# Scan of a hybrid SSD and attention layer: gated y kept in place, one norm per group, four transpositions moved into the next group

## The chip, the cores and the metric

The kernel runs on one core of one Trainium2 chip. Its time is the device time of one execution in microseconds (us); for each kernel the median of several executions is compared. The kernel before took 1962.46 us in the median of three runs (1960.18 to 1966.06).

## The reference

The layer takes a residual stream of 512 positions by 2048 channels. One input projection of the normalised stream feeds two branches, a bidirectional Mamba-2 scan (SSD) and a latent attention; both are projected, weighted, summed, projected again and added to the input. The change touches the end of the scan branch only, in float32:

```python
y_fwd = ssd_scan(xs, dtf, a_f, bm, cm)
y_bwd = flip(ssd_scan(flip(xs), flip(dtb), a_b, flip(bm), flip(cm)))
y = y_fwd + y_bwd + d_skip[:, None] * xs
y = y.reshape(b, s, D_SSM) * silu(z_ssm)
y = rmsnorm(y.reshape(b, s, SSM_GROUPS, D_SSM // SSM_GROUPS), ssm_norm_w)   # 4 groups of 512 channels
merged = sigmoid(g_ssm) * (y @ w_proj_ssm) + sigmoid(g_attn) * (o @ w_proj_attn)
```

`rmsnorm` divides each row of 512 channels by the root of its mean square plus 1e-6. The sequence is worked in four chunks of 128 positions.

## The kernel before

The program first normalises and transposes the input (`h_h`, `h_l`, a high and a low part, so that three products make one of float32), then makes the gates, then runs the scan as four groups of 512 channels (`ssd_group`, called for g = 0 to 3), then the attention and the output projections. The scan has little work for TensorE (PE); long products of the input projection are laid between its steps. They stand in a queue of generators (`Fill`), each a tile of 48 products (`xbc`, `qkv`, `za`; lines 169 to 171), and the program says after each step of the scan how many are run: `gap()` a planned share, `bit(n)` at least n. The order on PE is the order in which the program is written (PE is scheduled by hand); the other engines are ordered by the scheduler from the program order and from priorities (`tc.high_priority`), and every engine then works its list in order. An instruction that waits therefore holds all that stands behind it on its engine.

One group goes like this.

- First stretch. A `gap()`, then PE transposes the tile `BT` (`post_b`, line 1016) and, after six products each, four tiles `xs` (`post_x`). These go to PSUM tiles of the tag `pb`, of which there are two, used in turn. ScalarE (ACT) copies each out (`b_h`, line 1021; `xT`, line 1027), and VectorE (DVE) makes `b_l` from the first.
- State stretch. Three steps of the states (`loc`, `off`). ACT sets the accumulator `yo` to the skip term (line 1115, eight instructions), POOL adds to it (line 1094).
- Diagonal stretch. For each chunk c and half q a decay matrix `G` is made on DVE and ACT, and PE multiplies it with `xT` into `yb` (`diag`, line 1167). At q = 1 the chunk is whole: DVE adds `yo` and `yb` into a fresh tile `y` (line 1170, tag `yz`, two buffers), and `y_norm` follows at once: DVE multiplies by the gate `z` (line 965), ACT squares with a row sum (line 967), DVE scales the sum (line 968), `small_rsqrt` takes the root on ACT (line 186, which needs a table load of its own) and the reciprocal with one Newton step on DVE (lines 188 to 192), and ACT scales `y` (line 969).
- `y_turn` transposes a normalised chunk: four transpositions on PE into a `pb` tile (line 975), four scalings on ACT into `yt` (line 979) and one store from ACT's queue (line 289). A list `turns` holds chunks whose transposition is owed. Two are paid in the diagonal stretch, beside `diag`, one before the last `diag`, and the fourth in the next group's state stretch.

After groups 1 and 2 the program also takes the norm of the query or key/value latents (`r_sum`): PE sums the squares over partitions (line 353, tile `rp`), DVE adds the epsilon (line 355, tile `vv`, 128x512), and `small_rsqrt` works on all 512 columns (tiles `rt` and `rr`). After group 3 `fill.run(60)` and the last `y_turn` close the scan.

Of the kernel before, what the change touches and what calls it, by code (L numbers as in the profile page):

```python
# [12 lines left out]
F32 = mybir.dt.float32  # L13
F32R = mybir.dt.float32r
I32 = mybir.dt.int32
AF = mybir.ActivationFunctionType
ALU = mybir.AluOpType
AX = mybir.AxisListType

P = 128  # L20
D = 2048
SEQ = 512
KT = D // P
TT = SEQ // P
# [8 lines left out]
EPS = 1e-6  # L33
# [40 lines left out]
def build(tc, a):  # L74
    nc = tc.nc
    act, dve, pool, pe = nc.scalar, nc.vector, nc.gpsimd, nc.tensor
# [20 lines left out]
    hi = open_pool("hi", side="right")  # L97
# [4 lines left out]
    def few(n):  # L102

        n_small[0] += n
        assert n_small[0] <= 96
        return small[:, n_small[0] - n:n_small[0]]
# [76 lines left out]
    def small_rsqrt(v, n, new):  # L183

        t = new("rt")
        act.activation(t, v, AF.Sqrt)
        r = new("rr")
        dve.reciprocal(r, t)
        dve.tensor_mul(t, r, r)
        dve.tensor_mul(t, t, v)  # L190
        dve.tensor_scalar(t, t, -0.5, 1.5, ALU.mult, ALU.add)
        dve.tensor_mul(r, r, t)
        return r
# [10 lines left out]
    for t in range(TT):  # L204
# [3 lines left out]
        for i, cs in enumerate(slice(*e) for e in zip(edges, edges[1:])):  # L208
# [3 lines left out]
            if i == 0:  # L212
                most, v, root, r = (few(1) for _ in range(4))
# [189 lines left out]
    fill = Fill()  # L403
# [514 lines left out]
    sw = open_pool("sw", reuse_waits="tile")  # L918

    for tag, n, shape in (("r", 6, [P, SEQ]), ("da0", 2, [P, 4, P]), ("da1", 2, [P, 4, P]), ("E", 2, [P, 4, P]),  # L920
                          ("G", 2, [P, 4, P]), ("cbf", 2, [P, P]), ("cbb", 2, [P, P]),
                          ("yz", 2, [P, SEQ]), ("yo", 1, [P, TT, SEQ]), ("xT", 1, [P, TT, SEQ])):
        for _ in range(n):
            sw.tile(shape, F32R if tag == "r" else F32, tag=tag, bufs=n, name=f"{tag}_place")

# [16 lines left out]
    ssz = few(16)  # L942
# [8 lines left out]
                i = qkv_left.pop(0)  # L951
                fill.add("qkv", qkv_gen(i, sq_q if i < 6 else sq_kv, tmp2))

    def rsqrt1(v):

        return small_rsqrt(v, 1, lambda n: hi.tile([P, 1], F32, tag={"rt": "mx", "rr": "nm"}[n], bufs=4, name=n))

    def z_load(c, g):
        z = st("z")
        nc.sync.dma_start(z, zs_d[c][g])  # L960
        return z

    def y_norm(c, g, y, z):

        dve.tensor_mul(y, y, z)
        s_ = ssz[:, 4 * c + g:4 * c + g + 1]
        act.activation(z, y, AF.Square, accum_out=s_)
        dve.tensor_scalar(s_, s_, 1.0 / 512, EPS, ALU.mult, ALU.add)
        act.activation(y, y, AF.Copy, scale=rsqrt1(s_))

    def y_turn(c, g, y):

# [11 lines left out]
    turns = deque()  # L984
# [18 lines left out]
    def ssd_group(g):  # L1003
# [20 lines left out]
        def post_x(ct, xs):  # L1024
            def f():
                tp = transposed(xs)
                act.copy(xT[:, :, ct * P:(ct + 1) * P], tp.rearrange("p (c k) -> p c k", c=TT))
            return f
# [16 lines left out]
        def bit(n):  # L1045
            left[0] += n - fill.run(n)
# [6 lines left out]
            bit(9)  # L1053
        post_b()
        for ct in range(4):
            bit(6)
            post_x(ct, xss[ct])()

        yo = sw.tile([P, TT, SEQ], F32, tag="yo", name="yo")
        yoh = yo.rearrange("p c (h k) -> p c h k", h=HPG)  # L1060
# [49 lines left out]
        for i in range(3):  # L1110
            with tc.high_priority(offset=30):
                ss = [state(0, i, nxt[0]), state(1, 3 - i, nxt[1])]
            if i == 0:
                for j in range(HPG):
                    act.activation(yoh[:, :, j], xTh[:, :, j], AF.Copy, scale=dsk[:, g * HPG + j:g * HPG + j + 1])
            if i < 2:
                nxt = [state_in(0, i + 1), state_in(1, 2 - i)]
            gap()
            if turns:
                y_turn(*turns.popleft())  # L1120
            offdiag(0, i + 1, ss[0])
            offdiag(1, 2 - i, ss[1])
            if i == 2:
                cb_make(0)
            gap()
# [34 lines left out]
        def diag(c, q, G):  # L1160

            if q == 0:
                ybs[c] = pc("yb")
            yb = ybs[c]
            for j in range(4):
                cs = slice((q * 4 + j) * 64, (q * 4 + j + 1) * 64)
                pe.matmul(yb[:, cs], G[:, j, :], xT[:, c, cs], start=True, stop=True)
            if q == 1:
                y = sw.tile([P, SEQ], F32, tag="yz", bufs=2, name="y")
                dve.tensor_add(y, yo[:, c], yb)  # L1170
                with tc.high_priority(offset=30):
                    y_norm(c, g, y, zs.pop(c))
                turns.append((c, g, y))

        last = None
        da_load(0, 0)
        for c in range(TT):
            for q in range(2):
                G = seg_make(c, q)
                if q == 0 and c < TT - 1:  # L1180
                    cb_make(c + 1)
                if (c, q) != (TT - 1, 1):
                    da_load(c + q, 1 - q)
                if q == 1:
                    zs[c] = z_load(c, g)
                gap()
                if q == 1 and len(turns) > 1:
                    y_turn(*turns.popleft())
                if last:
                    diag(*last)  # L1190
                last = (c, q, G)
# [1 line left out]
            loaded[g + 1] = group_loads(g + 1)  # L1193
        gap()
        gap()
        y_turn(*turns.popleft())
        diag(*last)

        if g == 2:
            put(rkv_d, r_sum(sq_kv, KL, tmp2))  # L1200
# [5 lines left out]
        ssd_group(g)  # L1206
    add_fill("za", len(za_left))
    ahead[0] = 150
    fill.run(60)
    y_turn(*turns.popleft())  # L1210
    close_pool("sw")
    close_pool("sp")

# [653 lines left out]
```

## Time and profile before

| | |
|---|---|
| median of three runs | 1962.46 us (1960.18 to 1966.06) |
| the profiled execution | 1964.5 us |
| its span in the trace | 1962.7 us |
| granted TensorE clock, mean | 0.998 |
| the scan in the trace | about 560 to 1096 us |
| last `diag` of group 0, 1, 2, 3 starts at | 696.76, 827.56, 950.50, 1081.06 us |
| ACT table loads for the root (line 186) | 16, of 1.28 us each |

Times in rows of the trace are us from the span's start; a row of the timeline gives start, duration, engine, line, operation, tiles, shape and count, and in brackets how long the engine idled before it and what released it. Products on PE overlap: a product of 128x512 is recorded with 0.39 us, though the next starts 0.23 us later. So the cost of a product is the distance of starts, and a row of idle time on PE is a lower bound of a wait.

### The profile page before, as it was taken

What the parts mean: (1) busy time and instruction counts of PE and PEld (TensorE: products, weight loads), DVE (VectorE), ACT (ScalarE), POOL (GpSimd) and SP (SyncE); (2) the same over time, 40 slices, a digit from 0 to 9 for tenths busy, and PEclk for the clock granted to TensorE, in tenths of its full rate; (3) what the DMA queues carried; (4) which work ended last, traced back from release to release, by engine and by line L of the source; (5) the groups of instructions that cost most, each with busy time, mean ns of one, the idle gap of its engine ahead of it and who ended that gap; (6) DMA issues with size and microseconds to landing.
All of it is one profiled execution on the core that took longest, in us unless ns stands there. A gap on an engine that the chain in (4) does not pass through costs nothing.

```text
span 1962.7 us, 24515 instructions
## 1 busy us (share of the span) xinstructions
PE 1926.9 (98%) x8834; PEld 1592.1 (81%) x8834; DVE 1462.4 (75%) x2064; ACT 1038.3 (53%) x1536; POOL 248.3 (13%) x317
## 2 busy tenths in 40 slices
PE   7999999999999999999999999999999999999998
PEld 5888888888878888878888888888877788888886
DVE  7986676776759869799786557676776899879467
ACT  6444444444455866757757444444455455444344
POOL 0001001001112021030210211111021111100011
PEclk9999999999999999999999999999999999999999
DMA  5469669668654554665554867887389687846437
GB/s 211 164 206 261 161 166 249 153 183 240 145 178 145 174 165 153 216 186 178 178 158 150 235 186 204 211 217 203 103 220 317 222 286 284 285 159 241 160 90 169
DMA packets 145785, 383.27 MB, mean 195 GB/s; under 512 B 16704, under 2 KB 34304, under 8 KB 145472
## 3 DMA queue, kind: packets, MB, share of 16 engines
q1 hardware_dynamic: 79104, 234.02, 35.7%
q0 software_dynamic: 30912, 103.82, 23.4%
q10 hardware_dynamic: 35648, 43.87, 6.3%
q8 instruction: 69, 1.13, 0.2%
q14 instruction: 52, 0.43, 0.1%
HBM read 329.55 MB, written 98.17 MB: 218 GB/s over the span
## 4 chain that ended last, share of the span: by engine, by line
PE 80%; DVE 9%; DMA 5%; issue 3%; ACT 2%; POOL 0%; SPq 0%; DVEq 0%; POOLq 0%; ACTq 0%
PE P L605 11%; PE P L606 11%; PE P L604 11%; PE xbc L169 3%; PE xbc L170 3%; PE za L169 3%; PE xbc L171 3%; PE za L171 3%; PE za L170 3%; PE qkv L171 2%; DVE wl L459 2%; PE qkv L169 1%; PE f L1626 1%; PE f L1625 1%; PE f L1627 1%
## 5 line engine op out<-in xcount | busy, mean ns | idle before, releaser
L458 ACT CAST wh<-X 128x1024 fp32r<-128x1024 f32 x164 | 172.5, 1054 | 199.5 <-PE P L606 157.8
L459 DVE TENSOR_TENSOR wl<-X,wh 128x1024 fp32r<-128x1024 f32 x164 | 199.7, 1222 | 84.8 <-ACT wh L458 84.2
L165 DVE TENSOR_TENSOR wl<-wraw,wh 128x1024 fp32r<-128x1024 f32 (+2 forms) x150 | 174.1, 1163 | 83.6 <-ACT wh L164 78.2
L164 ACT CAST wh<-wraw 128x1024 fp32r<-128x1024 f32 (+2 forms) x150 | 144.5, 967 | 116.3 <-PE za L170 32.1
L459 DVE TENSOR_TENSOR wl<-Y,wh 128x1024 fp32r<-128x1024 f32 x88 | 107.5, 1223 | 66.4 <-ACT wh L458 66.3
L458 ACT CAST wh<-Y 128x1024 fp32r<-128x1024 f32 x88 | 92.6, 1054 | 115.6 <-PE P L606 101.3
L169 PE MATMUL xbc<-h_h,wh 128*128 128x512 f32 x384 | 153.6, 400 | 0.0
L171 PE MATMUL xbc<-h_h,wl 128*128 128x512 f32 x384 | 150.1, 391 | 0.0
L170 PE MATMUL xbc<-h_l,wh 128*128 128x512 f32 x384 | 150.0, 391 | 0.0
L604 PE MATMUL P<-wh,h_h 128*128 128x512 f32 x384 | 149.4, 389 | 0.0
L605 PE MATMUL P<-wl,h_h 128*128 128x512 f32 x384 | 149.4, 389 | 0.0
L606 PE MATMUL P<-wh,h_l 128*128 128x512 f32 x384 | 149.4, 389 | 0.0
L458 ACT CAST wh<-wraw 128x1024 fp32r<-128x1024 f32 x68 | 71.6, 1054 | 110.6 <-PE P L606 58.5
L459 DVE TENSOR_TENSOR wl<-wraw,wh 128x1024 fp32r<-128x1024 f32 x68 | 83.0, 1221 | 59.5 <-ACT wh L458 59.4
L605 PE MATMUL P<-wl,S 128*128 128x512 f32 x288 | 112.1, 389 | 0.8 <-DVE wl L459 0.8
L606 PE MATMUL P<-wh,S 128*128 128x512 f32 x288 | 112.0, 389 | 0.0
L604 PE MATMUL P<-wh,S 128*128 128x512 f32 x288 | 112.0, 389 | 0.0
L169 PE MATMUL za<-h_h,wh 128*128 128x512 f32 x256 | 101.7, 397 | 0.0
L171 PE MATMUL za<-h_h,wl 128*128 128x512 f32 x256 | 99.9, 390 | 0.0
L170 PE MATMUL za<-h_l,wh 128*128 128x512 f32 x256 | 99.7, 389 | 0.0
L1377 ACT ACTIVATE pr<-s,nm 128x512 f32<-128x512 f32 x64 | 44.0, 688 | 79.1 <-DVE nm L1375 79.1
L171 PEld LDWEIGHTS xbc<-h_h,wl 128*128 128x128 f32 x384 | 72.4, 188 | 15.7
(746 smaller groups left out, 5084.8 us busy)
## 6 DMA issues: line engine op xcount, KB each, us to landing
wraw<-wi SPq DMA_DIRECT2D x102, 512.0 KB, 3.6
T_wps<-wps POOLq DMA_DIRECT2D x32, 512.0 KB, 11.0
da<-da_d SPq DMA_DIRECT2D x64, 256.0 KB, 4.0
T_wpa<-wpa POOLq DMA_DIRECT2D x32, 512.0 KB, 9.1
wraw<-wps SPq DMA_DIRECT2D x24, 512.0 KB, 6.2
wraw<-wo SPq DMA_DIRECT2D x20, 512.0 KB, 3.6
xbc_d<-xbc ACTq DMA_DIRECT2D x24, 256.0 KB, 2.9
wraw<-wun SPq DMA_DIRECT2D x16, 384.0 KB, 5.4
```

The source lines that it names most:

```text
L164: act.copy(h, raw)
L165: dve.tensor_sub(l, raw, h.bitcast(F32))
L169: pe.matmul(out, wh, xh, start=start, stop=False)
L170: pe.matmul(out, wh, xl, start=False, stop=False)
L171: pe.matmul(out, wl, xh, start=False, stop=stop)
L458: i = act.copy(hi_, raw)
L459: dve.tensor_sub(lo_, raw, hi_.bitcast(F32))
L604: pe.matmul(bs[i], xh, wh, start=(j == 0), stop=False)
L605: pe.matmul(bs[i], xh, wl, start=False, stop=False)
L606: pe.matmul(bs[i], xl, wh, start=False, stop=(j == 7))
L1377: act.activation(pr, s, AF.Exp, bias=nm, scale=SCALE, accum_out=sm_)
L1625: pe.matmul(acc, mh, wh, start=(start and k == 0), stop=False)
```

## The change

`y` has no tile of its own any more. DVE adds `yb` into `yo[:, c]` in place and multiplies by `z` there; ACT squares it with a row sum, as before. Root, reciprocal and Newton step are left out per chunk. When the fourth chunk of a group is gated, `y_norms` takes them once for four columns (`ssz[:, 4g:4g+4]`, into `yr`), and ACT scales the four chunks one after another. All four chunks are then owed to `turns`. They are paid in the first stretch of the next group: after each of the four `post_x`, one `y_turn`; between two of them stand nine products in place of six (`bit(9 if g else 6)`). The places in the state stretch, in the diagonal stretch and before the last `diag` have none any more. After group 3, `fill.run(45)` comes before the first `y_turn` and `fill.run(6)` after each. Nothing is left out of the computation.

```diff
--- before.py
+++ after.py
@@ -919,7 +919,7 @@
 
     for tag, n, shape in (("r", 6, [P, SEQ]), ("da0", 2, [P, 4, P]), ("da1", 2, [P, 4, P]), ("E", 2, [P, 4, P]),
                           ("G", 2, [P, 4, P]), ("cbf", 2, [P, P]), ("cbb", 2, [P, P]),
-                          ("yz", 2, [P, SEQ]), ("yo", 1, [P, TT, SEQ]), ("xT", 1, [P, TT, SEQ])):
+                          ("yo", 1, [P, TT, SEQ]), ("xT", 1, [P, TT, SEQ])):
         for _ in range(n):
             sw.tile(shape, F32R if tag == "r" else F32, tag=tag, bufs=n, name=f"{tag}_place")
 
@@ -951,22 +951,25 @@
                 i = qkv_left.pop(0)
                 fill.add("qkv", qkv_gen(i, sq_q if i < 6 else sq_kv, tmp2))
 
-    def rsqrt1(v):
-
-        return small_rsqrt(v, 1, lambda n: hi.tile([P, 1], F32, tag={"rt": "mx", "rr": "nm"}[n], bufs=4, name=n))
-
     def z_load(c, g):
         z = st("z")
         nc.sync.dma_start(z, zs_d[c][g])
         return z
 
-    def y_norm(c, g, y, z):
+    def y_gated(c, g, y, z):
 
         dve.tensor_mul(y, y, z)
-        s_ = ssz[:, 4 * c + g:4 * c + g + 1]
-        act.activation(z, y, AF.Square, accum_out=s_)
-        dve.tensor_scalar(s_, s_, 1.0 / 512, EPS, ALU.mult, ALU.add)
-        act.activation(y, y, AF.Copy, scale=rsqrt1(s_))
+        act.activation(z, y, AF.Square, accum_out=ssz[:, 4 * g + c:4 * g + c + 1])
+
+    yr = [few(4), few(4)]
+
+    def y_norms(g, ys):
+        s4 = ssz[:, 4 * g:4 * g + 4]
+        dve.tensor_scalar(s4, s4, 1.0 / 512, EPS, ALU.mult, ALU.add)
+        r = small_rsqrt(s4, 4, lambda n: yr[n == "rr"])
+        for c, y in enumerate(ys):
+            act.activation(y, y, AF.Copy, scale=r[:, c:c + 1])
+            turns.append((c, g, y))
 
     def y_turn(c, g, y):
 
@@ -1053,8 +1056,10 @@
             bit(9)
         post_b()
         for ct in range(4):
-            bit(6)
+            bit(9 if g else 6)
             post_x(ct, xss[ct])()
+            if turns:
+                y_turn(*turns.popleft())
 
         yo = sw.tile([P, TT, SEQ], F32, tag="yo", name="yo")
         yoh = yo.rearrange("p c (h k) -> p c h k", h=HPG)
@@ -1116,8 +1121,6 @@
             if i < 2:
                 nxt = [state_in(0, i + 1), state_in(1, 2 - i)]
             gap()
-            if turns:
-                y_turn(*turns.popleft())
             offdiag(0, i + 1, ss[0])
             offdiag(1, 2 - i, ss[1])
             if i == 2:
@@ -1166,11 +1169,9 @@
                 cs = slice((q * 4 + j) * 64, (q * 4 + j + 1) * 64)
                 pe.matmul(yb[:, cs], G[:, j, :], xT[:, c, cs], start=True, stop=True)
             if q == 1:
-                y = sw.tile([P, SEQ], F32, tag="yz", bufs=2, name="y")
-                dve.tensor_add(y, yo[:, c], yb)
-                with tc.high_priority(offset=30):
-                    y_norm(c, g, y, zs.pop(c))
-                turns.append((c, g, y))
+                y = yo[:, c]
+                dve.tensor_add(y, y, yb)
+                y_gated(c, g, y, zs.pop(c))
 
         last = None
         da_load(0, 0)
@@ -1184,8 +1185,6 @@
                 if q == 1:
                     zs[c] = z_load(c, g)
                 gap()
-                if q == 1 and len(turns) > 1:
-                    y_turn(*turns.popleft())
                 if last:
                     diag(*last)
                 last = (c, q, G)
@@ -1193,8 +1192,9 @@
             loaded[g + 1] = group_loads(g + 1)
         gap()
         gap()
-        y_turn(*turns.popleft())
         diag(*last)
+        with tc.high_priority(offset=60):
+            y_norms(g, [yo[:, c] for c in range(TT)])
 
         if g == 2:
             put(rkv_d, r_sum(sq_kv, KL, tmp2))
@@ -1206,8 +1206,10 @@
         ssd_group(g)
     add_fill("za", len(za_left))
     ahead[0] = 150
-    fill.run(60)
-    y_turn(*turns.popleft())
+    fill.run(45)
+    while turns:
+        y_turn(*turns.popleft())
+        fill.run(6)
     close_pool("sw")
     close_pool("sp")
```

The scheduler's order shows the move. On PE, from the last `diag` of group 1 to the first stretch of group 2, before (`cst` is the identity in a transposition, the sum's matrix of ones in `rp`; `xbc` and `qkv` are products of the fill, of which only the first of a run is kept):

```order
L975 MATMUL turn<-cst,y 128x128 x4
L1167 MATMUL yb<-xT,G 128x64 x4
L353 MATMUL rp<-sq_q,cst 128x512
L169 MATMUL xbc<-h_h,wh 128x512
...
L1016 MATMUL pb<-cst,BT 128x128 x4
...
L1016 MATMUL pb<-cst,xs 128x128 x4
...
L1016 MATMUL pb<-cst,xs 128x128 x4
```

And the same place now:

```order
L1170 MATMUL yb<-xT,G 128x64 x4
L353 MATMUL rp<-sq_q,cst 128x512
L169 MATMUL xbc<-h_h,wh 128x512
...
L1019 MATMUL pb<-cst,BT 128x128 x4
...
L1019 MATMUL pb<-cst,xs 128x128 x4
L978 MATMUL turn<-cst,yo 128x128 x4
...
L1019 MATMUL pb<-cst,xs 128x128 x4
L978 MATMUL turn<-cst,yo 128x128 x4
```

The transposition of a gated chunk now stands right behind the first `xs`. Between the last `diag` and `BT` stand 12 products in both (15 after groups 0 and 2), between `BT` and the first `xs` six before and nine now.

On DVE, the same place before, from the addition of the last chunk on:

```order
L1170 TENSOR_TENSOR y<-yo,yb 128x512
L355 TENSOR_SCALAR vv<-rp 128x512
L965 TENSOR_TENSOR y<-y,z 128x512
L188 RECIPROCAL rr<-rt 128x512
L968 TENSOR_SCALAR small<-small 128x1
L1022 TENSOR_TENSOR b_l<-pb,b_h 128x512
L189 TENSOR_TENSOR rt<-rr 128x512
L188 RECIPROCAL rr<-rt 128x1
L165 TENSOR_TENSOR wl<-wraw,wh 128x1024
L189 TENSOR_TENSOR rt<-rr 128x1
```

And now, from the epsilon of `r_sum` to the last step of the four-column reciprocal (the rows on `small` are `y_norms`, those on `rr`, `rt` and `vv` are `r_sum`):

```order
L355 TENSOR_SCALAR vv<-rp 128x512
L968 TENSOR_SCALAR small<-small 128x4
L188 RECIPROCAL rr<-rt 128x512
L188 RECIPROCAL small<-small 128x4
L1025 TENSOR_TENSOR b_l<-pb,b_h 128x512
L189 TENSOR_TENSOR small<-small 128x4
L189 TENSOR_TENSOR rt<-rr 128x512
L190 TENSOR_TENSOR small<-small 128x4
L190 TENSOR_TENSOR rt<-rt,vv 128x512
L191 TENSOR_SCALAR small<-small 128x4
L191 TENSOR_SCALAR rt<-rt 128x512
L192 TENSOR_TENSOR small<-small 128x4
```

The two chains are interlaced in both, and the 512-column reciprocal stands ahead of the small one in both; after group 2 the order is the same, with one `wl` (line 165) inside.

On ACT, the same place now:

```order
L962 ACTIVATE z,small<-yo 128x512
L186 ACT_TABLE_LOAD
L186 ACTIVATE rt<-vv 128x512
L186 ACTIVATE small<-small 128x4
L1024 CAST b_h<-pb 128x512
L1030 COPY xT<-pb 128x4x128
L971 ACTIVATE yo<-yo,small 128x512 x4
L289 DMA rq_d<-rr 128x512
L982 ACTIVATE yt<-turn,vec 128x128 x4
```

The four scalings stand in a row, behind the first `xT` copy and ahead of the first four scalings into `yt`. After group 0 there is no `r_sum`; there the order is the square, `b_h`, the table load, the root, one `wh` cast (line 164), the four scalings, and then the first `xT` copy.

## The prediction

> **What bounds the kernel now.** I read the page first, then the waits of PE inside the scan, then the rows around the end of a group.
>
> ```profile
> PE 1926.9 (98%) x8834; PEld 1592.1 (81%) x8834; DVE 1462.4 (75%) x2064; ACT 1038.3 (53%) x1536; POOL 248.3 (13%) x317
> PE 80%; DVE 9%; DMA 5%; issue 3%; ACT 2%; POOL 0%; SPq 0%; DVEq 0%; POOLq 0%; ACTq 0%
> ```
>
> PE is busy for 98% of the span and carries 80% of the chain that ended last. Work taken from ACT or DVE is worth nothing by itself here; what counts is whether PE waits more or less. In the window of the scan (560 to 1140 us) its waits are these:
>
> ```profile
> PE pb L1016 <- ACT dec L346: 2.6, 1, 2.6
> PE qkv L171 <- DVE wl L165: 2.1, 2, 1.3
> PE off L170 <- DVE s_l L1085: 0.7, 1, 0.7
> ```
>
> The first stands at the very start of the scan, which the change leaves as it is. So all that a lighter ACT and DVE could give back is 2.1 + 0.7 = 2.8 us. Of what the change can take there is no such limit: every wait that it puts into PE's list counts in full, since the products behind it are only shifted.
>
> **PE's side of the new place.** The change removes no product and no transposition from PE. It moves four transpositions per group to the next group's first stretch. The first is the one to look at: it needs the first scaled chunk, and that needs the square of the last chunk. When would PE get there? The rows of PE after groups 0, 1 and 2:
>
> ```profile
> 696.76 1.00 PE L1167 MATMUL yb<-xT,G 128*128 128x64 f32 x8
> ...
> 701.11 0.60 PE L1016 MATMUL pb<-cst,BT 128*128 128x128 f32 x4
> 702.94 0.60 PE L1016 MATMUL pb<-cst,xs 128*128 128x128 f32 x4
> ...
> 827.12 0.60 PE L975 MATMUL turn<-cst,y 128*128 128x128 f32 x4
> 827.56 1.00 PE L1167 MATMUL yb<-xT,G 128*128 128x64 f32 x8
> ...
> 832.06 0.60 PE L1016 MATMUL pb<-cst,BT 128*128 128x128 f32 x4
> 833.89 0.60 PE L1016 MATMUL pb<-cst,xs 128*128 128x128 f32 x4
> ...
> 955.69 0.60 PE L1016 MATMUL pb<-cst,BT 128*128 128x128 f32 x4
> 957.52 0.60 PE L1016 MATMUL pb<-cst,xs 128*128 128x128 f32 x4
> ```
>
> ```profile
> 641.30 0.39 PE L169 MATMUL xbc<-h_h,wh 128*128 128x512 f32 x1
> 641.53 0.39 PE L170 MATMUL xbc<-h_l,wh 128*128 128x512 f32 x1
> ```
>
> A product takes 0.23 us from start to start. From `BT` to the first `xs`, with six products, it is 1.83 us in all three places; with nine it becomes 1.83 + 3 x 0.23 = 2.5. Four transpositions take 827.56 - 827.12 = 0.44 us. On the clock of these rows PE reaches the first moved transposition at 701.11 + 2.5 + 0.44 = 704.1 after group 0, at 835.0 after group 1, at 958.6 after group 2. (The transposition that stood ahead of the last `diag` is gone, but that shifts both sides.)
>
> **The norm's side, after group 0.**
>
> ```profile
> 702.35 1.28 ACT L186 ACT_TABLE_LOAD   x1
> 703.65 0.20 ACT L186 ACTIVATE rt<-small 128x1 f32<-128x1 f32 x1
> 704.22 1.05 ACT L164 CAST wh<-wraw 128x1024 fp32r<-128x1024 f32 x1
> 705.17 0.73 ACT L969 ACTIVATE y<-y,rr 128x512 f32<-128x512 f32 x1
> 704.66 0.16 DVE L192 TENSOR_TENSOR rr<-rr,rt 128x1 f32<-128x1 f32 x1
> ```
>
> The order on both engines is the same up to the root, so the small reciprocal is ready at 704.66 + 0.16 = 704.8. On ACT the `wh` cast now follows the root directly and ends about 703.85 + 1.05 = 704.9. The first scaling takes 0.73: chunk 0 is ready at 705.6. PE waits 1.5 us. Behind this stand three more scalings, one `xT` copy and four scalings into `yt`, and only then is the `pb` tile free that the second `y_turn` needs: 704.9 + 4 x 0.62 + 0.5 + 1.14 (the four `yt`, row below) = 709.0. PE wants it at 705.6 + 0.44 + 2.5 = 708.6, and waits 0.4. I take 2.0 us, bounds 1.2 and 2.6.
>
> ```profile
> 698.23 1.14 ACT L979 ACTIVATE yt<-turn,vec 128x128 f32<-128x128 f32 x4
> ```
>
> **After group 1** the latents' norm shares the engines.
>
> ```profile
> 830.51 0.68 DVE L355 TENSOR_SCALAR vv<-rp 128x512 f32<-128x512 f32 x1
> 831.11 0.68 DVE L965 TENSOR_TENSOR y<-y,z 128x512 f32<-128x512 f32 x1
> ...
> 834.33 3.35 DVE L188 RECIPROCAL rr<-rt 128x512 f32<-128x512 f32 x1 [2.54 <-ACT rt L186]
> ```
>
> ```profile
> 832.37 1.28 ACT L186 ACT_TABLE_LOAD   x1 [2.20 <-issue]
> 833.66 0.63 ACT L186 ACTIVATE rt<-vv 128x512 f32<-128x512 f32 x1
> ```
>
> The gate's product now stands ahead of `vv` and ends about 831.6; the square ends at 832.4, the table load at 833.7, and the wide root starts where it does now. So does the reciprocal of 512 columns, 3.35 us long, and the small one stands behind it in DVE's list. How long the rest takes is read after group 2, where the same chain ran without a disturbance:
>
> ```profile
> 957.12 3.38 DVE L188 RECIPROCAL rr<-rt 128x512 f32<-128x512 f32 x2 [2.04 <-ACT rt L186]
> ...
> 961.74 1.22 DVE L165 TENSOR_TENSOR wl<-wraw,wh 128x1024 fp32r<-128x1024 f32 x1
> 962.87 0.14 DVE L191 TENSOR_SCALAR rt<-rt 128x1 f32<-128x1 f32 x1
> ...
> 963.53 0.15 DVE L192 TENSOR_TENSOR rr<-rr,rt 128x1 f32<-128x1 f32 x1
> 963.65 0.43 DVE L191 TENSOR_SCALAR rt<-rt 128x512 f32<-128x512 f32 x1
> 964.11 0.69 DVE L192 TENSOR_TENSOR rr<-rr,rt 128x512 f32<-128x512 f32 x1
> ```
>
> From the start of the wide reciprocal to the end of the small chain: 963.68 - 957.12 = 6.56. After group 1 there is no `wl` in between (962.87 - 961.74 = 1.13 less), but one wide step more stands ahead (964.11 - 963.65 = 0.46): 5.9 us. So the four factors are ready at 834.35 + 5.9 = 840.3, the first scaling at 841.0, and PE, which stood ready at 835.0, waits 6.0 us. Bounds 5.0 and 8.5: in the present run the same steps ended only at 843.6, beside a slow one:
>
> ```profile
> 841.25 2.37 DVE L192 TENSOR_TENSOR rr<-rr,rt 128x512 f32<-128x512 f32 x2
> ```
>
> With 0.2 for the second `pb` tile: 6.2.
>
> **After group 2** the `wl` stays inside. On ACT the `yt` scalings of an older chunk no longer stand ahead of the root, so I let its table load start 0.4 us before the present 955.16, and the wide reciprocal with it:
>
> ```profile
> 955.16 1.28 ACT L186 ACT_TABLE_LOAD   x1
> ```
>
> The wide reciprocal starts at 956.7, the factors are ready at 956.7 + 6.56 + 0.46 = 963.7, chunk 0 at 964.4. PE stood ready at 958.6: 5.8 us, with the second tile 5.9. Bounds 5.0 and 6.5.
>
> **After group 3** 45 products (10 us) stand ahead of the first `y_turn`, and the chain, which took 705.9 - 696.8 = 9.1 us without `r_sum`, is hidden. But on ACT a `wh` cast (1.05), a table load (1.28) and a Silu (0.6) stand inside the first chunk's `yt` scalings. The third `y_turn` needs that `pb` tile 2 x 1.83 = 3.7 us after the first; ACT is done 0.5 + 0.55 + 1.05 + 1.28 + 0.6 + 0.55 = 4.5 us after it. 0.8 us, bounds 0 and 1.5.
>
> **The clock.** One wait of this size is in the trace already, the one of 2.6 us at the start:
>
> ```profile
> 574.00:576.00 2.00, 0.00 (x0) 0.00 (x0) 0.00 (x0) 1.97 (x4) 1.26 (x1) 0.99 1.02 406
> 576.00:578.00 2.00, 1.65 (x6) 1.55 (x7) 1.19 (x3) 1.27 (x4) 0.00 (x0) 0.50 0.06 23
> 578.00:580.00 2.00, 2.00 (x10) 1.53 (x9) 0.00 (x0) 1.00 (x3) 0.00 (x0) 0.65 0.00 0
> 924.00:926.00 2.00, 0.98 (x5) 0.48 (x3) 2.00 (x5) 1.96 (x4) 0.00 (x0) 1.00 0.89 275
> ```
>
> Behind PE's busy time and the others stands the granted clock: it fell to 0.50 and came back within 4 us. What PE did in that time cost 1.65 x 0.50 + 2.00 x 0.35 = 1.5 us more. The wait of 1.3 us at 924 us left it at 1.00. So I add 1.5 us to each of the two long waits (bounds 0 and 3), and nothing to the 1.5 us after group 0, which is nearer to the second (bounds 0 and 1.5). The Trainium skill, "TensorE: Matmul & The Clock Gate", section "What's actually happening", has the clock fall after one idle window of about 3.4 us, the windows running free; here it fell after 2.6 us, so the trace disagrees, and by the page a wait of 6 us would hold a whole window only about three times in four (an estimate from that page), 2.3 us in place of 3.0.
>
> **What is given back.**
>
> ```profile
> L186 ACT ACT_TABLE_LOAD x16 | 20.5, 1283 | 2.5 <-issue 2.2
> ```
>
> ACT is rid of 12 of the 16 table loads for the root, and DVE of 12 small chains; the waits of 2.8 us above stand where both were full. I take half of it, 1.4, bounds 0 and 2.8. The Trainium skill, "ScalarE: Activation LUTs", section "What ACT_TABLE_LOAD costs", adds a drain of about 1.38 us to each load of 1.28; the root at 703.65 starts right behind the load at 702.35, so the trace shows none, and by the page each of three waits would be 1.4 longer.
>
> **The sum.** 2.0 + 6.2 + 5.9 + 0.8 + 3.0 - 1.4 = 16.5 us. Against the profiled execution's 1964.5 that is 1981.0; the median of the runs is 2.0 below it, so 1979.0.
>
> **The rivals.**
>
> *The clock stays up.* The waits come, but the fill's products resume without a fall. For it: at 924 us it held. Against it: 2.6 us were enough at 574. 16.5 - 3.0 = 13.5: 1976.0.
>
> *A second wait in the state stretch.* The accumulator can be set anew only when the old one is transposed, so its eight instructions on ACT move behind the last `y_turn`, and the casts of the state queue up among them. For it: the second state's cast stands behind five of them in ACT's list, about 2 us. Against it: there are some 6 us of products between `loc` and the second `off`. If it comes in each of three groups at 2.5 us, 24: 1986.5.
>
> *No wait.* The norm is ready in time, or the products ahead cover it. For it: nothing in the rows after groups 1 and 2, where the present chain of one column ended at 963.68, 5 us after PE would stand ready. 1962.5.
>
> *Faster.* The norm is in time and the relief of ACT and DVE removes the 2.8 us and some lags too small for the list of waits; it decides from the point where the chain from the last `diag` to chunk 0 takes less than the 7.3 us (704.1 - 696.8) that PE needs to the first moved transposition. It took 9.1 without `r_sum`. Minus 5: 1957.5.
>
> **How the numbers follow.** Forecast 0.63, clock stays up 0.15, second wait 0.10, no wait 0.07, faster 0.05. The low end of the sum's bounds is 1.2 + 5.2 + 5.1 + 0 + 0 - 2.8 = 8.7, which gives 1971.2; the high end, with 2.6 + 8.7 + 6.6 + 1.5 + 4.5 (a fall after each of three waits) - 0 = 23.9, gives 1986.4 and takes in the second wait. The range is 1971 to 1987. About 0.3% (6 us) is what a measurement of this kernel can tell from no change: slower 0.88, within 0.07, faster 0.05.
>
> **What would show it.** In the profile after, PE's waits in the scan should have a group of the transposition waiting for ACT's scaling of `yo`, three times, some 14 us in all and 6 us the longest, with the granted clock at half behind the long ones. Table loads for the root should be 4. If that group is missing or below 3 us, the step that fails is the time at which PE reaches the transposition or the order on DVE; if it is there and the time is not 10 us longer, the waits were paid elsewhere before.

## The result, and the profile after

The changed kernel takes 1990.66 us in the median of five runs (1985.34 to 1996.98); the kernel before took 1963.39 us in five runs on the same chip. The ratio is 1.0131, 95% interval 1.0116 to 1.0146: slower by 27.3 us, where 16.5 had been forecast. The direction was right, the size was not: the range ended at 1987. One later execution of the changed kernel, at a mean granted clock of 0.753, took 2431 us; no figure below takes it in.

The page of the changed kernel (the profiled execution took 1997.0 us): its first line and the lines on the engines and on the chain that ended last:

```profile
span 1995.2 us, 24402 instructions
PE 1940.3 (97%) x8834; PEld 1600.7 (80%) x8834; DVE 1457.3 (73%) x1992; ACT 1012.7 (51%) x1505; POOL 251.4 (13%) x317
PE 80%; DVE 8%; DMA 7%; issue 3%; ACT 2%; POOL 0%; SPq 0%; ACTq 0%; DVEq 0%; POOLq 0%
```

ACT is busy for 26 us less and DVE for 5 us less, and the span is 32 us longer. DMA's share of the chain rose from 5% to 7%: a first sign that not only the norm is late. PE's waits in the scan and just behind it (560 to 1200 us; us in total, times, longest), the first seven rows:

```profile
PE turn L978 <- ACT yo L971: 12.6, 3, 5.9
PE pb L1019 <- ACT dec L346: 2.6, 1, 2.6
PE za L171 <- DVE wl L165: 1.8, 1, 1.8
PE loc L170 <- DVE xw_l L1074: 1.6, 1, 1.6
PE loc L169 <- ACT xw_h L1073: 1.3, 1, 1.3
PE turn L978 <- ACT yt L982: 1.0, 2, 0.9
PE loc L169 <- DVE tmp L1098: 0.8, 1, 0.8
```

The first row is the forecast: the first moved transposition waits for ACT's scaling of `yo`, three times. The second stood there before. The rows of `loc` (the state stretch, whose inputs are the tiles `xw`) and `za` (the fill behind the scan) were not forecast.

A list of waits misses what PE loses at a low clock. The next table therefore counts all of it: for each matmul of PE, the time to the start of the next one less the usual spacing of its kind (the median, 0.23 us for a product of 512 columns), summed over stretches. "Again" is a second profile of the same kernel, from the first experiment.

| stretch of the span, us | what lies there | before | after | again |
|---|---|---|---|---|
| 700 to 750 | first stretch of group 1 | 0.4 | 2.7 | 2.6 |
| 800 to 850 | first stretch of group 2 | 1.0 | 9.2 | 8.9 |
| 950 to 1000 | first stretch of group 3 | 0.6 | 8.8 | 8.6 |
| 850 to 900 | state stretch of group 2 | 1.7 | 8.3 | 4.8 |
| 1100 to 1200 | end of the scan, first loads of the attention | 0.0 | 5.2 | 8.3 |
| 750 to 800 and 900 to 950 | diagonal stretches of groups 1 and 2 | 3.6 | 1.1 | 0.9 |

The first three rows lose 18.7 us against before, the next two 11.8 (11.4 in the second profile), and the last gives 2.5 back. Of what is left of the 32 us between these two profiles, 2.9 lie in one low clock near 120 us, before the scan, which the second profile does not have in that size.

The granted clock in four windows of the changed kernel (us, then busy time and instructions of PE, PEld, DVE, ACT and POOL, the granted clock, DMA share, GB/s):

```profile
838.20:844.40 6.20, 0.35 (x4) 0.11 (x2) 6.00 (x11) 1.41 (x3) 0.00 (x0) 0.88 0.00 0
844.40:851.20 6.80, 6.80 (x25) 5.69 (x26) 1.23 (x1) 4.82 (x12) 0.00 (x0) 0.61 0.33 107
975.20:980.70 5.50, 0.23 (x4) 0.02 (x1) 5.47 (x12) 1.91 (x4) 0.00 (x0) 0.89 0.10 20
980.70:987.50 6.80, 6.80 (x25) 5.69 (x26) 0.29 (x1) 3.79 (x11) 0.00 (x0) 0.59 0.39 140
```

In the first and third, PE stands idle while DVE works through the norms. In the two behind them PE is busy throughout and gets 25 instructions done at a mean clock of 0.6. Where no long wait stands ahead, a stretch of the same length holds 39, as in the run with the reciprocal behind the norm, after group 0.

### The profile page after: what moved, and what is told of

Its sections match the earlier page's. It is cut to its first block, busy times and chain, and to the rows that moved or that the text cites. A ratio compares the mean times of both kernels' runs of the same rounds, so it can differ in the third digit from the quotient of the medians.

```text
span 1995.2 us, 24402 instructions
## 1 busy us (share of the span) xinstructions
PE 1940.3 (97%) x8834; PEld 1600.7 (80%) x8834; DVE 1457.3 (73%) x1992; ACT 1012.7 (51%) x1505; POOL 251.4 (13%) x317
## 4 chain that ended last, share of the span: by engine, by line
PE 80%; DVE 8%; DMA 7%; issue 3%; ACT 2%; POOL 0%; SPq 0%; ACTq 0%; DVEq 0%; POOLq 0%
PE P L605 11%; PE P L606 11%; PE P L604 11%; PE xbc L169 3%; PE xbc L170 3%; PE xbc L171 3%; PE za L169 2%; PE za L171 2%; PE za L170 2%; PE qkv L169 2%; PE qkv L171 2%; PE qkv L170 2%; PE f L1627 1%; PE f L1629 1%; PE f L1628 1%
## 5 line engine op out<-in xcount | busy, mean ns | idle before, releaser
L170 PEld LDWEIGHTS xbc<-h_l,wh 128*128 128x128 f32 x384 | 73.4, 191 | 14.8 <-issue 0.2
```

Source lines behind the costliest of these rows:

```text
L170: pe.matmul(out, wh, xl, start=False, stop=False)
```

## The experiments

Ratios are to runs of the kernel before on the same chip in the same batch.

| kernel | median us | ratio, 95% interval |
|---|---|---|
| the changed kernel again | 1991.2 | 1.0132 (1.0115 to 1.0149) |
| reciprocals into the diagonal stretch | 1992.9 | 1.0145 (1.0129 to 1.0160) |
| four sums of y held | 1985.6 | 1.0104 (1.0087 to 1.0121) |
| both | 1985.4 | 1.0108 (1.0093 to 1.0124) |
| all sums behind the first head | 1984.4 | 1.0087 (1.0071 to 1.0104) |
| the same, norm per chunk | 1972.5 | 1.0033 (1.0022 to 1.0043) |
| all sums behind the first head, reciprocal behind the norm | 1974.3 | 1.0038 (1.0025 to 1.0051) |
| kernel before, all sums behind the first head | 1964.3 | 0.9996 (0.9984 to 1.0008) |
| all sums behind the first head, transpositions later | 1971.3 | 1.0032 (1.0019 to 1.0044) |
| the same, reciprocal behind the norm | 1968.3 | 1.0017 (1.0006 to 1.0028) |
| the last one with six products | 1969.6 | 1.0030 (1.0018 to 1.0041) |
| six products, norm per chunk, reciprocal where the change has it | 1970.0 | 1.0022 (1.0013 to 1.0030) |

Three causes were to be told apart. Theory 1: the group's norm is late, with the latents' reciprocal ahead of it. Theory 2: POOL's list holds the state inputs (`xw`) up. Theory 3: the attention's first loads (tile `raw`) land late.

### Which waits come back

No edit.

> The changed kernel unaltered, profiled a second time, to see which of its waits come back. Theory 1 (norm of four chunks late, reciprocal of the compressed norm ahead of it) and theory 2 (a copy on POOL's list waits ahead of the state inputs of the third group) both expect about 1990.7 us, PE waits of about 1.6, 6.0 and 5.4 us at the first transposition of groups 1, 2 and 3, a low clock behind the two long ones, and some 5 us of PE waits near 883 to 893 us. Rival (noise of one execution): the waits near 883 us, the one of 1.9 us at 1153 us and the low clock near 130 us are gone.

The waits of PE in the second profile, same window:

```profile
PE turn L978 <- ACT yo L971: 12.6, 3, 5.9
PE za L171 <- DVE wl L165: 4.4, 1, 4.4
...
PE loc L169 <- DVE tmp L1098: 1.9, 1, 1.9
```

The first row is the same to 0.1 us. The two unforeseen places are there again, with other sizes (4.4 for 1.8 us at the weight, 1.9 for 3.7 at the state inputs). All three belong to the kernel.

### The reciprocals into the diagonal stretch

```diff
-        if g == 2:
-            put(rkv_d, r_sum(sq_kv, KL, tmp2))
-        if g == 1:
-            put(rq_d, r_sum(sq_q, QL, tmp2))
...
                 last = (c, q, G)
+                if (c, q) == (1, 0) and g > 1:
+                    put(*((rq_d, r_sum(sq_q, QL, tmp2)) if g == 2 else (rkv_d, r_sum(sq_kv, KL, tmp2))))
```

> The changed kernel with the compressed norms' wide reciprocals taken out of the group ends and put into the middle of the next group's diagonal stretch; nothing else moved by hand. Theory 1: the waits at the first transposition fall from 6.0 and 5.4 us to the 1.6 us of group 1, where no reciprocal stands ahead, and no low clock follows: 4.4 + 3.8 + 2 x 2.9 = 14 us less, about 1977 us. Rival (the scaling of four chunks is late by itself, whatever stands ahead): the waits stay above 4 us and the time above 1986 us. Theory 2 alone would leave the time at 1990 us, and its waits near 883 us stay here.

The waits of PE, 560 to 1250 us:

```profile
PE turn L978 <- ACT yo L971: 4.7, 3, 1.8
PE loc L169 <- ACT xw_h L1073: 4.3, 1, 4.3
PE za L171 <- DVE wl L165: 3.6, 1, 3.6
PE yb L1170 <- DVE G L1160: 3.0, 2, 2.6
PE loc L170 <- DVE xw_l L1074: 2.6, 3, 1.3
...
PE qkv L171 <- DVE wl L165: 1.9, 1, 1.9
```

The forecast of theory 1 for the place came true: 12.6 us of waits became 4.7, the longest 1.8. The forecast for the time did not: 1992.9 us. The wide reciprocal now stands in a stretch where DVE has no slack (`yb` waits 2.6 us for `G`, `qkv` 1.9 us for a weight), and the state inputs, reached earlier, wait longer: 4.3 and 1.3 us where it was 1.3 and 1.6. The gain was paid elsewhere.

### The sums of y held

```diff
-            pool.tensor_add(yo[:, c], yo[:, c], tmp)
+            last_off[:] = [pool.tensor_add(yo[:, c], yo[:, c], tmp)]
...
+    with tc.issue_after(last_off[0].ins):
         for step in sums(yn_d, slice(0, 2048)):
             for f in step:
                 f()
```

> The changed kernel with the four transfers that sum the stored y (the POOL copies and the accumulating one) held behind the scan's last instruction of POOL; nothing else moved by hand. Theory 2: the cluster of PE waits near 883 to 893 us goes, about 7 us less, 1983.5 us; the waits of 6.0 and 5.4 us stay. Rival (that cluster comes from ACT and DVE, late after the wait of 5.4 or 6.0 us and the low clock): the cluster stays and the time is about 1990 us. If the held transfers are missed later, up to 17 us come back behind the scan.

POOL's instructions in the state stretch of group 2, first of the changed kernel, then of the kernel before (start, length, instruction, and in brackets the idle time ahead of it and what ended it):

```profile
864.44 1.11 POOL L1420 DMA_DIRECT2D yn_S<-yn_x  x1
...
881.46 0.54 POOL L1417 DMA_DIRECT2D yn_S<-yn_S  x1 [10.47 <-DMA yn_S<-yn_x]
...
883.25 2.05 POOL L1070 TENSOR_TENSOR xw<-xT,wst 128x512 f32<-128x512 f32 x2
```

```profile
855.44 3.03 POOL L1065 TENSOR_TENSOR xw<-xT,wst 128x512 f32<-128x512 f32 x2
...
860.21 1.11 POOL L1418 DMA_DIRECT2D yn_S<-yn_x  x1
872.32 0.51 POOL L1415 DMA_DIRECT2D yn_S<-yn_S  x1 [11.00 <-DMA yn_S<-yn_x]
```

The stored chunks of `y` are summed in DRAM by transfers on POOL's queue. A copy of such a sum cannot be issued until the accumulating transfer has landed, 17.0 us after its issue (881.46 - 864.44), and POOL stands still for the last 10.47 us of it. In the kernel before POOL stands still about as long (11.00 us), but behind the last two `xw`. In the changed kernel the chunks of group 1 are stored together in the first stretch of group 2, so the sums become due while state inputs are still to come, and the copy stands ahead of the last two `xw`. PE needs them, through the casts, from 883.6 on.

With the sums held, that wait is gone from PE's list, which has 12.6 us at the transpositions, 2.9 at a weight behind the scan, and nothing of `loc`. The stretch from 850 to 900 us falls from 8.3 (4.8 in the second profile) to 1.1. The ratio falls from 1.0132 to 1.0104, 5.5 us. These two intervals overlap a little; the same edit beside the moved reciprocals (next run) takes the ratio from 1.0145 to 1.0108, with the intervals apart. Theory 2 holds.

### Both edits

The two diffs above together.

> Both edits together (reciprocals in the middle of the next group, sums of y held). If the two causes are independent, the gains add: 14 + 7 = 21 us less than the changed kernel, about 1969.5 us, and what is left above the kernel before is the three waits of 1.6 us and the 3.5 us near 1153 us. If the POOL cluster was a consequence of the late group ends, the gain is that of the first edit alone, about 1977 us.

1985.4 us, neither 1969.5 nor 1977, and no less than with the sums held alone, as the run with the reciprocals alone already implies: `yb` waits 2.7 us for `G` and `qkv` 1.9 us for a weight here too, and the low clock behind them takes the rest. The gains do not add, because the edit of the reciprocals moved its cost, not because the causes depend on each other.

### All sums behind the first head

```diff
-            pool.tensor_mul(pace, sm_, sm_)
+            paced[:] = [pool.tensor_mul(pace, sm_, sm_)]
...
-    for step in sums(yn_d, slice(0, 2048)):
-        for f in step:
-            f()
+    y_late = [f for step in sums(yn_d, slice(0, 2048)) for f in step]
...
+        if hd == 1:
+            with tc.issue_after(paced[0].ins):
+                for f in y_late:
+                    f()
```

> The changed kernel with all seven transfers that sum the stored y issued behind the first head of the attention, so that none stands between POOL's scan work and none moves data while the attention's first loads arrive. Theory 2: as in the run that held four of them, the cluster near 883 us goes (1985.6 us there). Theory 3 (the wait of 1.9 to 4.6 us for a weight's low part near 1145 us comes from loads of raw that land in 11.5 us where it was 7.6 us before, because two accumulating transfers of 1 MB run beside them): that wait of about 3 us and the low clock behind it (1.5 to 3 us) go too, about 1981 us. Rival to theory 3 (raw loads are simply issued later, since four transpositions instead of one hold their place): the wait stays and the time is 1985.6 us.

There are eight such transfers, not seven. The last line of the view of the tile `raw` gives the time from issue to landing of its ten loads: in the kernel before, in the run with four sums held, and in this one (the changed kernel's median is 11.0).

```profile
DMA to landing us min/median/max: 5.2/7.6/10.4
```

```profile
DMA to landing us min/median/max: 6.3/11.5/14.0
```

```profile
DMA to landing us min/median/max: 2.7/5.8/7.7
```

DVE's list in the changed kernel shows what a late load does there:

```profile
1144.63 1.46 DVE L1237 SCALAR_TENSOR_TENSOR raw<-raw,vec,R 128x512 f32<-128x512 f32 x2
1152.34 0.75 DVE L1237 SCALAR_TENSOR_TENSOR raw<-raw,vec,R 128x512 f32<-128x512 f32 x1 [6.24 <-DMA raw<-qkv_d]
1153.00 1.29 DVE L1239 TENSOR_TENSOR cq_l<-raw,cq_h 128x512 fp32r<-128x512 f32 x2
1154.21 1.22 DVE L165 TENSOR_TENSOR wl<-wraw,wh 128x1024 fp32r<-128x1024 f32 x1
```

DVE waits 6.2 us for one load of `raw`, and the weight's low part that PE needs stands behind it. With the sums out of the way the loads land in 5.8 us, PE's wait for `za` is gone from its list, and the stretch from 1100 to 1200 us falls from 5.8 us (four sums held) to 1.1. In that view theory 3 is borne out, but in a narrower form than it was put. In the kernel before, two accumulating transfers (1108.55 us on) also run beside the last four loads (1108.57 us on), and PE does not wait. What the change adds is a later start: the first load is issued 25.4 us behind the last `diag` (1131.03 - 1105.67) where it was 15.0 (1096.03 - 1081.06). With the sums away it is issued as late, 25.6 us behind, and PE does not wait either. So neither the late start nor the sums alone make the wait; the two together do.

The step in time is 1.2 us by the medians and 3.3 by the ratios, whose intervals overlap: too small to be told from nothing. A part of the gain is paid again at the sums' new place, as the control below shows.

### The norm per chunk, in the new place

```diff
-                y_gated(c, g, y, zs.pop(c))
+                with tc.high_priority(offset=30):
+                    y_gated(c, g, y, zs.pop(c))
+                    y_norm1(c, g, y)
...
-        with tc.high_priority(offset=60):
-            y_norms(g, [yo[:, c] for c in range(TT)])
```

`y_norm1` is the norm of the kernel before on `yo[:, c]`; it also appends the chunk to `turns`. All sums stay behind the first head.

> As the run with all sums behind the first head, but the norm of y taken per chunk again, as in the kernel before (a root, a reciprocal and a scaling behind each chunk); y stays in place and the transpositions stay in the next group's first stretch. Theory 1 (it is the norm at the group's end that is late, not the place of the transpositions): the three waits of 1.6, 6.0 and 5.4 us and the low clock behind the two long ones go, 14 + 2 x 2.9 = 20 us less than the run with the sums behind the first head, about 1961 to 1965 us. Rival (the place is too early for anything): the last chunk still keeps PE waiting, 3 to 6 us per group, 1970 us or more. What the twelve more roots and their table loads cost on ACT shows as what is above 1961 us.

The waits of PE, 560 to 1200 us:

```profile
PE pb L1020 <- ACT dec L346: 2.9, 1, 2.9
PE turn L978 <- ACT yt L982: 1.8, 2, 1.0
PE turn L978 <- ACT xT L1031: 1.6, 2, 1.0
PE za L171 <- DVE small L970: 1.6, 1, 1.6
```

No transposition waits for a scaling of `yo` any more, and the time falls by 11.9 us, to 1972.5. The norm at the group's end was what was late. But 1961 to 1965 us had been expected, and it is 7.5 us above 1965.0. Of these, 3.4 us are two transpositions that wait for ACT to empty a `pb` tile of `x` (L1031) and two that wait for one of `y` (L982), as eight transposed tiles per stretch now pass through the same two tiles.

### The reciprocal behind the norm

```diff
-        dve.tensor_mul(r, r, t)
+        normed[:] = [dve.tensor_mul(r, r, t)]
         return r
...
+        if g in (1, 2):
+            with tc.issue_after(normed[0].ins):
+                put(*((rq_d, r_sum(sq_q, QL, tmp2)) if g == 1 else (rkv_d, r_sum(sq_kv, KL, tmp2))))
```

> As the run with all sums behind the first head, with the compressed norm's reciprocal ordered on DVE directly behind the group norm instead of ahead of it. Theory 1: waits of 1.6 us at all three groups and no low clock, 14 us less than the run with the sums behind the first head, about 1967 us. Rival (as when the reciprocals stood in the diagonal stretch: what is moved displaces other work of DVE): the gain at the first transposition is there, and 3 us or more come back as PE waits for a weight's low part or for xw_l in the state stretch.

The waits of PE, 560 to 1200 us, and the granted clock behind the first moved transposition after groups 0 and 1:

```profile
PE turn L980 <- ACT yo L973: 3.8, 3, 1.4
PE turn L980 <- ACT yt L984: 2.6, 4, 1.2
PE pb L1022 <- ACT dec L348: 2.3, 1, 2.3
PE off L170 <- DVE s_l L1093: 1.6, 4, 0.7
```

```profile
704.60:711.40 6.80, 6.63 (x39) 5.53 (x40) 0.37 (x1) 5.19 (x14) 0.00 (x0) 1.00 0.46 148
836.70:843.50 6.80, 5.60 (x30) 4.59 (x31) 4.42 (x3) 5.93 (x14) 0.00 (x0) 1.00 0.13 39
```

Each of the three waits is now about 1.3 us, as after group 0, and the clock stays at full speed behind them: from 1984.4 to 1974.3 us, 10.1 us of the 14 expected. Once the reciprocal alone is taken from ahead of the norm, without another stall in its place, theory 1 gives its gain. Most of the rest is in the second and fourth rows: 4.2 us of waits for `yt` and `s_l`, which come to 1.0 + 0.3 in the run it starts from.

### The kernel before with the sums behind the first head

> The kernel before, with the seven transfers that sum y behind the first head of the attention and nothing else. Control for theory 2: in the kernel before these transfers stand behind the state inputs and cost PE at most the 1.2 us near 862 us, so 1963 to 1964.5 us, no difference that can be measured. If it is faster by more than 2 us, the sums cost something in the kernel before too, and the gains of the held runs are not the change's.

1964.3 us against 1965.0, ratio 0.9996: no difference. To move the sums gains the kernel before nothing that can be measured; their price in the changed kernel (5.5 us for the four that were held first, 8.8 by the ratios for all, 1.0132 against 1.0087) comes from the moment at which the change makes them due.

The new place has a price of its own. POOL's rows behind the first head, ACT's row that waits for the last of them, and PE's wait behind it, in this run:

```profile
1225.81 0.53 POOL L1416 DMA_DIRECT2D yn_S<-yn_S  x1 [9.62 <-DMA yn_S<-yn_x]
1234.02 1.01 POOL L1419 DMA_DIRECT2D yn_S<-yn_x  x1 [7.68 <-DMA yn_S<-yn_S]
1234.69 0.56 POOL L1383 TENSOR_TENSOR small<-sm__10313 128x1 f32<-128x1 f32 x1
```

```profile
1235.29 0.69 ACT L1378 ACTIVATE pr<-s,nm 128x512 f32<-128x512 f32 x1 [8.80 <-POOL small L1383]
```

```profile
PE pb L1391 <- DVE pr L1380: 1.1, 1, 1.1
```

A small instruction of POOL (L1383), by which the program paces its loads, stands behind the sums' transfers; ACT waits 8.8 us for it before the next exponential (`pr`), and PE 1.1 us behind that. All eight runs with the sums behind the first head have this wait, 0.9 to 2.0 us on PE and 8.6 to 9.7 us on ACT; the six others have none there. It is theory 2's mechanism again, in another place.

### The transpositions later in the same stretch

```diff
             post_x(ct, xss[ct])()
-            if turns:
-                y_turn(*turns.popleft())
+        while turns:
+            bit(9)
+            y_turn(*turns.popleft())
```

> As the run with all sums behind the first head (1984.4 us), with the four transpositions of y moved behind the four of x in the same first stretch, each behind nine products, so that the first one comes some 9 us later; the reciprocal stays ahead of the group norm. Theory 1 in its narrow form (the norm is ready a fixed time after the group's end and whoever asks 9 us later finds it done): the waits of 1.6, 6.0 and 5.4 us, the second waits behind the bank of x and the low clock go, about 14 + 6 = 20 us less, 1964 to 1966 us. Rival (the lateness moves on: y's space is free later, the state stretch starts with late sums of y and late casts): 3 us or more per group come back in the state stretch, 1972 us or more.

> As the run with the later transpositions, and with the reciprocal behind the group norm, and nine instead of six products behind each transposition after the last group. If the later place alone covers the norm, the reciprocal's place no longer matters: 1964 to 1966 us, like the run beside it, less at most the 1 us of the wait after the last group. If the later place leaves a part of the 6 us uncovered, this run is faster than the one beside it by that part. Against the kernel before: no difference that can be measured, since nothing that the change takes away (twelve roots and their table loads on ACT) stood on PE's path.

The waits of PE, 560 to 1200 us, in the first of the two and in the second:

```profile
PE pb L1020 <- ACT dec L346: 2.1, 1, 2.1
PE yb L1172 <- DVE G L1162: 2.1, 1, 2.1
PE turn L978 <- ACT yt L982: 0.9, 1, 0.9
```

```profile
PE pb L1022 <- ACT dec L348: 2.4, 1, 2.4
PE yb L1174 <- DVE G L1164: 2.1, 1, 2.1
```

The narrow form of theory 1 holds: asked some 9 us later, the norm is there, and not one transposition in the scan's groups waits for it, wherever the reciprocal stands. The times are 1971.3 and 1968.3, not 1964 to 1966: one new wait of 2.1 us for `G` at the end of group 2, with a low clock behind it, and the wait for `pr` behind the first head (1.1 and 1.8 us). The wait of 0.9 us after the last group goes with nine products between the transpositions.

### Six products, and the norm per chunk beside it

```diff
-            bit(9 if g else 6)
+            bit(6)
...
-            bit(9)
+            bit(6)
```

> As the run with later transpositions and the reciprocal behind the norm (1968.3 us), with six products instead of nine behind each of the eight transpositions of the first stretch, so that 24 products of each group go back to the later gaps. If the wait of 2.2 us that came up near 944 us for G of the third group's last chunk was the price of those products (the diagonal stretch too short of them), it shrinks to under 0.5 us and its low clock goes: about 1964.5 us, the kernel before within 0.15%. If the wait has another cause, 1968 us again. If six are too few to cover the norm, up to 1.5 us per group come back at the first transposition.

> The same places and products as the run beside it, but the norm of y per chunk again. It isolates what the norm once per group is worth: twelve table loads and twelve chains of small instructions less. If these cover or delay nothing that PE waits for, the two runs agree within 2 us; if DVE's and ACT's freed time counts, the run beside it is faster by more than that; if the late norm still costs, this one is faster.

The wait for `G` did go, but `loc` then waits for `xw_l` (3.2 us in two places in the first run, 2.3 in the second); that the state stretch now comes too soon would explain it, and is not shown. 1969.6 and 1970.0 us: no gain from the 24 products, and no difference between the norm once per group and per chunk. The two runs differ in one thing more than was set down for them: the second leaves the latents' wide reciprocal where the changed kernel has it (at 829.54 us, ahead of the last chunk's small one), the first puts it behind the norm (836.47 us). With the transpositions this late, the norm once per group and the reciprocal behind it are together worth nothing that these runs can tell; the norm alone was not run at this place. None of the versions of the changed kernel beats the kernel before; the nearest is 0.17% slower.

## Why the prediction fell short, by its own steps

**What bounds the kernel: right.** ACT lost 12 table loads and 26 us of busy time, and the last two runs, one with the norm per chunk, take the same time.

**The waits after groups 0, 1 and 2: right.** Forecast 1.5, 6.0 and 5.8 us at the first transposition; the starts of PE give 1.6, 6.0 and 5.4. The chain behind them is the one read out of the trace of before. The rows of DVE in the changed kernel:

```profile
837.65 3.35 DVE L188 RECIPROCAL rr<-rt 128x512 f32<-128x512 f32 x1 [1.77 <-ACT rt L186]
840.92 0.12 DVE L188 RECIPROCAL small<-small 128x4 f32<-128x4 f32 x1
...
843.39 0.15 DVE L192 TENSOR_TENSOR small<-small 128x4 f32<-128x4 f32 x1
```

From the start of the wide reciprocal to the end of the small chain it is 843.54 - 837.65 = 5.9 us, the figure of the prediction. The runs that took the reciprocal from ahead of the norm cut the long waits to 1.8 us and less; those that took the norm per chunk, or came later, removed them.

**The clock: right in kind, too small.** The step took 1.5 us for each long wait, from one fall of 2.6 us of idling. Behind the waits of 6.0 and 5.4 us the half clock lasted twice as long, 6.83 us in place of 3.41; products stood 0.427 us apart in place of 0.23. From the first moved transposition to the second it took 5.52 us (844.35 to 849.87) and 5.60 (980.69 to 986.29), where from the second to the third it took 2.95: 2.6 us are lost each time, 5.2 for a term of 3.0, still inside its bound of 3 each. The rival "the clock stays up" is refuted. The Trainium skill, "TensorE: Matmul & The Clock Gate", section "What's actually happening", has the full clock come back after one busy window of about 3.4 us, windows running free; with that the trace agrees here: the half clock, from 842.94 to 849.77 us, ran on through the window of 3.41 us in which PE resumed (844.35) and through one whole busy window behind it.

**After group 3: failed.** "0.8 us, bounds 0 and 1.5" counted the third transposition, which did wait 1.0. It did not ask what the four late transpositions do to the transfers behind them: the first loads of the attention start some 10 us later behind the last `diag` than before, beside accumulating transfers of 1 MB, and hold DVE up with a weight behind them. Measured 5.2 to 8.3 us in that stretch. The step followed the moved transpositions as far as ACT's scalings, and not on to the stores and to the loads and sums behind them.

**A second wait in the state stretch: the rival that came, for another reason.** It had been put down to ACT, at 2.5 us in each of three groups, with a chance of 0.10. It came in one group, at 3.1 to 6.6 us, from POOL: a transfer's wait ahead of the state inputs. The sums' transfers stood on POOL's list in the trace of before (rows above), with 11 us of standing still; the forecast gave them no term. With them held back the loss of that stretch fell from 8.3 us to 1.1.

**What is given back: right in size, the reason not borne out.** Forecast 1.4 of at most 2.8; the diagonal stretches gave 2.5. The reason given was ACT's and DVE's relief from 12 table loads and small chains. But the row of `qkv` waiting for a weight's low part (2.1 us in the kernel before) is also missing from the list of the last run, which takes the norm per chunk with 15 table loads for the root. What that run shares with the change is that no transposition stands in the diagonal stretch; that this is the reason is not shown, and the size was luck.

**The sum.** In the forecast's own grouping, measured against before in the profile: first stretches with their clock 18.7 (17.1 forecast), end 5.2 (0.8), state stretch 6.6 (0), given back 2.5 (1.4). That makes 28.0 where 16.5 stood, and 26.8 in the second profile, for 27.3 in the medians. Nearly all that was missed is the two places where the changed moment of the stores of `y` meets other work: 11 us by this count of one profile, of which the run with all sums moved won back 8.8 by the ratios.

What stays open: the 3 to 8 us by which the repaired versions are slower than the kernel before. A part of it is the sums' new place, with 0.9 to 2.0 us of waits. Their other waits are shown, each with its place, but they change with every small shift, and no run here isolates one of them.

## What to carry to other kernels

When a step that ends in a store is moved, follow the store: who reads it, on whose queue that reader waits, and what stands behind it there. Here some 11 of 27 us were lost beside transfers that the diff does not touch, and sent to another place these transfers held up what stood behind them there. And a wait that an edit removes is only won if the instruction that caused it lands where its engine has slack: the reciprocal moved into the diagonal stretch gave back all that it had gained, and placed directly behind the norm it gained 10 us.

## What the runs showed of the hardware

The half clock came in pieces of 3.41 us. Behind the waits of 5.4 and 6.0 us it lasted two of them, in each of the four profiles that have these waits; behind the wait of 2 to 3 us at the start of the scan one piece came in five of the fourteen profiles, and none in the others, for the same rows of PE. And a copy that needs an accumulating transfer of 1 MB in DRAM held POOL's list until 17.0 us after that transfer's issue (12.1 in the kernel before, 14.1 in the second profile of the changed kernel, 20.3 in the run with the reciprocals moved): an instruction of POOL that stands behind the copy waits with it (10.47 us of standing still in the changed kernel, 11.00 in the kernel before).
